# A decoder layer on eight cores: DMAs and side work placed by modelled PE time instead of where they are issued

## Chip, cores, metric

One Trainium2 chip, two dies of four cores; all eight cores run the same program on different data (two cores share a sequence of 4096 tokens, each produces 2048 output tokens). The metric is the device time of the slowest core, in microseconds (us). Some executions fall in a slower state, in which the cores of one die or of both show a lower granted clock.

PE is TensorE, DVE VectorE, ACT ScalarE, POOL GpSimd, SP the SyncE queue that issues plain DMAs. `ws` is the scratch copy of the weights in bf16, `wst` the fp32 original, one *unit* 128 x 2048 elements.

## The reference, cut to what matters

```python
h = rmsnorm(x, norm_mix_pre)
q, k, v, u, g_attn, g_pool = split(h @ w_in)
y_attn = stick_breaking_attention(q, k, v) @ w_attn_branch      # strictly causal, 8 heads of 128
y_pool = (pool_group(multiscale_causal_pool(u)) * pool_scale) @ w_pool_branch
x = x + rmsnorm((sigmoid(g_attn) * y_attn + sigmoid(g_pool) * y_pool) @ w_out, norm_mix_post)
h = rmsnorm(x, norm_ffn_pre)
gate, val = split(causal_depthwise_conv(h @ w_up))              # width 3: needs two earlier tokens
x = x + rmsnorm((gelu(gate) * val) @ w_down, norm_ffn_post)
x = x + rmsnorm(sigmoid(x @ w_ple_gate) * (p @ w_ple), norm_ple_post)
```

## The kernel before

A core works through four stages, which I call A to D. **A**: eight chunks of 512 tokens are normed, transposed and projected to K and V (chunks 4 to 7, its own, to Q too); with chunks 5 to 7 the attention of its first tile is interleaved, which begins with a *halo*, the attention of just two earlier tokens, needed by the convolution. **B**: four mixers (gates, branches, pooling, output projection), interleaved with the attention of the next tile. **C**: FFN up and down, twice. **D**: the per-layer embedding (PLE).

A small tracker in Python records which instruction last wrote or read each region and emits semaphore waits. In the traces an instruction that waits holds all that its engine has queued behind it: in the prediction's lines a norm's small step on POOL stands behind weight conversions, and PE waits 298 us for it. Small chains (norm, transpose, residual) lie in a list `side` and are popped after so much modelled PE time.

The parts that matter, with cuts:

```python
# weights: fp32 -> bf16, DRAM to DRAM, all 88 early units at the start, four to a DMA; POOL issues them
conv_units(list(range(U_V, U_U)), 4)
conv_units(list(range(U_U, U_UP)), 4)          # s_cv is a ring of 8 semaphores: the 9th waits for the 1st
def rstd(c_in, c_out):                         # part of every norm, on POOL too
    P.op("pool", ... tensor_scalar ...); P.op("pool", ... pow ...)

# end of the V projection of a chunk: V shifted by one row, minus V
P.dma("sp", s_v[0], [(Vs[0:127], Vv[1:128]), ...])
for hh in range(2):
    P.op("dve", ... Vsh - Vb ...)              # DVE's queue waits here for the copy

# halo: the load is issued at its use
for h in range(NH):
    kb_ = ldk(cc, h)
    P.op("pe", lambda e: e.matmul(bank(b), qh..., kb_.v(), ...), reads=[kb_.r(), qh.r()], ...)

# output projection, last block of a column group
for q_, ns in enumerate(mmq(pieces, [s[1].r() for s in sl] + [mxT.r()], [bkr(b)])):
    if lastb:
        W.done(sl[q_][0])                      # frees slot q_ and at once issues the next load into it
    yield ns                                   # ... but the next quarter declares all four slots as read
```

## Time and profile before

| | before |
|---|---|
| median of 16 runs | 6075.4 us |
| fast runs, all rounds | 6025 to 6112 us |
| cores of the profiled run | 6029.0 to 6081.7 us, clock 0.866 to 0.873 |
| PE busy | 4509.1 us, 74% of the span |
| stage A (to the last matmul before the first mixer) | 1736 us |
| stage B (to the first FFN matmul) | 1916 us |
| stage C (to the last FFN matmul) | 2037 us |
| stage D (rest) | 393 us |

How to read it: PE's work fills 74%, so a quarter of the time is waits, and the question is what each is for. The stage bounds are the first or last instructions of the source lines that belong to the stage. The lines are in the prediction.

### The profile page before, as it was taken

Reading aid. Unit: us, or ns where it says so; the run is one execution under the profiler, and the core shown is the slowest. Engines: PE = TensorE matmul, PEld = TensorE weight load, DVE = VectorE, ACT = ScalarE, POOL = GpSimd, SP = SyncE. Lnnn points to the kernel's source line nnn. Section 1 sums busy time; section 2 is a strip of 40 time slices with the busy share of each in tenths; the row PEclk is TensorE's granted clock in tenths of the full one; section 3 lists DMA queues with packets and bytes.
Section 4 is the critical chain, followed back from the end, with each engine's and each line's share of the span. In section 5 each row is a group of like instructions: output and inputs, shape, how many; then the busy total and the mean of one; then the engine's idle time right before and its main releaser. Section 6 shows DMA issues by size and latency. Waiting matters only on the chain.

```text
span 6081.7 us, 73291 instructions; the slowest of 8 cores (6029.0 to 6081.7 us)
## 1 busy us (share of the span) xinstructions
PE 4509.1 (74%) x25250; PEld 2351.5 (39%) x25664; DVE 2279.7 (37%) x2149; ACT 1855.4 (31%) x3066; POOL 220.4 (4%) x494
## 2 busy tenths in 40 slices
PE   1012645455779968967986867999988899998588
PEld 0001322223437624534543324666443344443233
DVE  0000211114747628847872214444221444411133
ACT  1000111103646526635762103333111333311122
POOL 1000000000000000000000000000000011100000
PEclk7566877778989979989997988999999999999697
DMA  9994223433357747746665833222454222247554
GB/s 165 109 110 85 67 65 112 142 112 123 113 148 187 176 123 195 188 129 187 179 170 147 199 114 117 74 77 77 139 191 159 91 77 77 77 144 211 145 152 132
DMA packets 328143, 803.31 MB, mean 132 GB/s; under 512 B 94826, under 2 KB 207914, under 8 KB 306090
## 3 DMA queue, kind: packets, MB, share of 16 engines
q1 hardware_dynamic: 317140, 663.02, 34.6%
q0 software_dynamic: 10640, 135.57, 15.7%
q8 instruction: 213, 3.49, 0.2%
q14 instruction: 150, 1.23, 0.1%
HBM read 823.40 MB, written 217.58 MB: 171 GB/s over the span
## 4 chain that ended last, share of the span: by engine, by line
PE 62%; DMA 18%; another core or an unknown queue 7%; SPq 5%; DVE 4%; issue 3%; ACT 2%; POOL 0%; DVEq 0%; ACTq 0%; POOLq 0%
PE PS L420 25%; PE PS L1239 20%; PE PS L1289 8%; SPq L202 4%; DMA SB<-ws 4%; DMA SB<-SB 3%; DMA SB<-xr 3%; PE PS L801 2%; PE PS L763 2%; PE PS L834 2%; DMA SB<-X 2%; DMA SB<-DVS 2%; DMA X<-SB 1%; DVE SB L519 1%
## 5 line engine op out<-in xcount | busy, mean ns | idle before, releaser
L420 PE MATMUL PS<-SB 128*128 128x512 bf16 (+3 forms) x9427 | 2131.4, 373 | 344.5 <-DMA SB<-ws 176.7
L420 PEld LDWEIGHTS PS<-SB 128*128 128x128 bf16 x9656 | 915.7, 101 | 1223.3 <-issue 596.3
L1239 PE MATMUL PS<-SB 128*128 128x342 bf16 (+1 forms) x6982 | 1227.6, 337 | 33.1 <-DVE SB L1034 29.9
L691 DVE TENSOR_TENSOR_SCAN SB<-SB 128x512 bf16<-128x512 f32 (+1 forms) x836 | 972.2, 1200 | 183.2 <-ACT SB L774 137.5
L439 ACT ACTIVATE SB<-PS 128x512 bf16<-128x512 bf16 (+5 forms) x1017 | 610.5, 605 | 1397.5 <-PE PS L534 430.0
L1239 PEld LDWEIGHTS PS<-SB 128*128 128x128 bf16 x7040 | 684.1, 97 | 574.6 <-issue 33.5
L534 PE MATMUL PS<-SB 128*128 128x128 bf16 x1024 | 94.0, 264 | 874.8 <-DVE SB L519 749.3
L1289 PE MATMUL PS<-SB 128*128 128x512 bf16 x2757 | 627.8, 388 | 26.8 <-DMA SB<-ws 12.6
L513 ACT ACTIVATE SB<-SB 128x512 bf16<-128x512 f32 (+3 forms) x245 | 216.9, 885 | 1386.6 <-DVE SB L443 815.0
L443 DVE COPY SB<-PS 128x512 f32<-128x512 f32 (+3 forms) x197 | 135.0, 687 | 1105.9 <-PE PS L1289 493.7
L774 ACT ACTIVATE SB<-PS 128x512 f32<-128x512 f32 (+1 forms) x832 | 475.4, 573 | 127.9 <-PE PS L763 64.0
L1263 DVE SCALAR_TENSOR_TENSOR SB<-SB 128x1024 f32<-128x1024 f32 x176 | 226.2, 1285 | 640.2 <-ACT SB L1256 640.2
L519 DVE SCALAR_TENSOR_TENSOR SB<-SB 128x2048 f32<-128x2048 f32 (+2 forms) x98 | 229.9, 2346 | 622.7 <-POOL SB L508 619.3
L534 PEld LDWEIGHTS PS<-SB 128*128 128x128 bf16 x1024 | 83.5, 121 | 895.0 <-issue 888.3
L1289 PEld LDWEIGHTS PS<-SB 128*128 128x128 bf16 x2816 | 280.5, 100 | 370.7 <-issue 76.6
L1253 ACT ACTIVATE SB<-PS 128x1026 f32<-128x1026 f32 (+1 forms) x176 | 180.5, 1025 | 744.0 <-PE PS L1239 737.9
L763 PE MATMUL PS<-SB 128*128 128x512 bf16 (+3 forms) x809 | 302.7, 376 | 124.7 <-ACT SB L774 66.2
L801 PE MATMUL PS<-SB 128*128 128x128 bf16 x3136 | 317.1, 222 | 3.7 <-DVE SB L691 1.4
L834 PE MATMUL PS<-SB 128*128 128x512 bf16 (+3 forms) x916 | 300.1, 351 | 24.6 <-DMA SB<-DVS 21.7
L801 PEld LDWEIGHTS PS<-SB 128*128 128x128 bf16 x3136 | 246.6, 99 | 180.8 <-issue 18.6
L1266 DVE SCALAR_TENSOR_TENSOR SB<-SB 128x1024 f32<-128x1024 f32 x176 | 226.1, 1285 | 19.1 <-DVE SB L1263 0.9
L443 DVE CAST SB<-PS 128x512 bf16<-128x512 f32 (+2 forms) x151 | 97.7, 649 | 340.0 <-PE PS L420 241.1
(53 smaller groups left out, 1393.8 us busy)
## 6 DMA issues: line engine op xcount, KB each, us to landing
SB<-ws SPq DMA_DIRECT2D x696, 512.0 KB, 3.7
ws<-wst POOLq DMA_DIRECT2D x66, 1024.0 KB, 10.3
SB<-xr SPq DMA_DIRECT2D x48, 1024.0 KB, 5.8
ws<-wst POOLq DMA_DIRECT2D x22, 2048.0 KB, 154.8
X<-SB SPq DMA_DIRECT2D x32, 1024.0 KB, 4.8
SB<-X SPq DMA_DIRECT2D x32, 1024.0 KB, 7.9
SB<-KS SPq DMA_DIRECT2D x240, 128.0 KB, 3.8
SB<-DVS SPq DMA_DIRECT2D x240, 128.0 KB, 3.8
```

What stands on the lines that cost most here:

```text
L202: e.dma_start(out=o, in_=i).then_inc(h, 16)
L420: ins = e.matmul(o, l, r, start=(start and a + i == 0), stop=(a + i == n - 1), skip_group_check=True)
L439: P.op("act", lambda e: e.activation(out=dst, in_=src, func=AF.Copy), reads=reads, writes=writes)
L443: P.op("dve", lambda e: e.tensor_copy(dst, src), reads=reads, writes=writes)
L519: P.op("dve", lambda e: e.scalar_tensor_tensor(out=dst, in0=xv, scalar=cv, in1=gv, op0=ALU.mult, op1=ALU.mult), reads=[xr_, small.r(col, c ...
L691: P.op("dve", lambda e: e.tensor_tensor_scan(out=pb.v(lo, NT), data0=gb.v(lo, NT), data1=mask, initial=init, op0=ALU.mult, op1=ALU.max), r ...
L763: P.op("pe", lambda e: e.matmul(bank(bk, NT - lo, lo), q_.v(b_ * 128, (b_ + 1) * 128), kb_.v(lo, NT), start=True, stop=True), reads=[kb_.r ...
L774: P.op("act", lambda e: e.activation(out=gb.v(lo, NT), in_=bank(bk, NT - lo, lo), func=AF.Sigmoid, scale=-QSCALE), reads=[bkr(bk)], writes ...
L801: ins = e.transpose(at[:, q_ * 128:(q_ + 1) * 128], src[q_].v(kb * 128, (kb + 1) * 128), ident)
L834: ins = e.matmul(o_, l, r, start=(first and i == 0), stop=False, skip_group_check=True)
L1239: ins = e.matmul(bank(bs[bi], c1 - c0), w3[:, k, :], hT2v[:, k, c0:c1], start=(k == 0), stop=(k == 15), skip_group_check=True)
L1289: ins = e.matmul(bank(b), actb[kk].v(q_ * 512 + blk * 128, q_ * 512 + (blk + 1) * 128), w3[:, k, :], start=(kk == 0), stop=(kk == NF - 1), ...
```

## The change

Its intent is to let PE run without holes, by giving each DMA and each side instruction a place in modelled time. The arithmetic is the same. The core of the diff (cuts are marked; memory layout and renaming are left out):

```diff
+        def after(ns, f, reads=(), writes=()):        # f is emitted ns of modelled PE time later; until
+            h = Hold(...)                             # then a conflicting access makes it fire first
+            timers.append((now[0] + ns, ...))
+        def dma_after(ns, q, sem, pairs, reads, writes):
+            after(ns, lambda: P.dma(q, sem, pairs, reads=reads, writes=writes), reads, writes)
...
-        conv_units(list(range(U_V, U_U)), 4)
-        conv_units(list(range(U_U, U_UP)), 4)
+        conv.extend(range(U_V, U_UP, 2))
+        def conv_every(ns, due=None):                 # two units, gated on PE's present count
+            if conv:
+                convert(conv[0], conv[0] + 2, ("pe", P.esem["pe"], P.cnt["pe"]))
+                conv.popleft()
+                after(due + ns - now[0], lambda: conv_every(ns, due + ns))
+        conv_every(11500)                             # 25000 in the mixers, 20000 from FFN up on
...
-            P.dma("sp", s_v[0], [(Vs[0:127], Vv[1:128]), ...
+            P.dma("sp", s_v[0], [(Vs[0:112], Vv[1:113]), (Vs[112:127], Vv[113:128]), ...
+            after(2000, t1, ...); after(11000, t2, ...); after(16500, t3, ...)   # copy, subtract, store
...
-                    for q_, ns in enumerate(mmq(pieces, [s[1].r() for s in sl] + [mxT.r()], [bkr(b)])):
+                    for q_, ns in enumerate(mmq(pieces, lambda a, sl=sl: [sl[a // 4][1].r(), mxT.r()], [bkr(b)])):
...
+        load_h2(0)                                    # FFN's input is loaded before the last mixer,
+        stats.append(run(mixer(3)))                   # and FFN up follows it without a drain
...
-                    P.dma("sp", s_st[4], [(H3[tb], st.v())], ...)    # FFN no longer transposes for PLE;
+            after(12000, lambda: tr3(n, xb), writes=[h3seq[n].r()])  # PLE does, one block ahead
-            P.dma("pool", s_wg[cg], [..., wsrc[cg])], ...)           # gate weights cast at their load
+            P.dma("sp", s_wg[cg], [..., ws[U_PG + cg * 4:...])], ...) # converted earlier
```

Besides, x loads run two blocks ahead, K, Q and residual stores are issued by `dma_after`, and `att_total` gets the true length of the attention, so that it ends with its mixer.

## The prediction

> **What bounds the kernel now.** I read the cores first: 6029.0 to 6081.7 us on all eight, clock 0.866 to 0.873, both dies alike, so this is the fast state. Then the page's head and slices.
>
> ```profile
> span 6081.7 us, 73291 instructions; the slowest of 8 cores (6029.0 to 6081.7 us)
> PE 4509.1 (74%) x25250; PEld 2351.5 (39%) x25664; DVE 2279.7 (37%) x2149; ACT 1855.4 (31%) x3066; POOL 220.4 (4%) x494
> ...
> PE   1012645455779968967986867999988899998588
> PEclk7566877778989979989997988999999999999697
> DMA  9994223433357747746665833222454222247554
> ```
>
> PE is the busiest engine, but only 74%, and each slice (152 us) in which it is low also has a low clock. The first eleven slices are poor, the middle is mixed, the end is good but for two dents. So this is no kernel with one bound; I asked for stretches instead.
>
> ```profile
> 50.00:660.00 610.00, 134.03 (x662) 64.27 (x675) 36.94 (x34) 33.24 (x41) 12.95 (x30) 0.61 0.81 104
> 660.00:1090.00 430.00, 222.38 (x1223) 107.71 (x1243) 63.32 (x67) 56.35 (x71) 9.64 (x26) 0.76 0.30 97
> 1090.00:1736.00 646.00, 395.55 (x2296) 194.90 (x2343) 238.50 (x229) 203.96 (x384) 5.19 (x14) 0.80 0.35 114
> ...
> 3750.00:4355.00 605.00, 592.23 (x4029) 389.95 (x4029) 264.80 (x208) 224.87 (x208) 15.45 (x83) 0.99 0.27 85
> ```
>
> (Columns: stretch, length, busy PE, weight loads, DVE, ACT, POOL, clock, DMA share, GB/s.) The projection phase up to 660 us has DMA at 0.81 and PE at a fifth; from there to 1736 us neither is full, so something serialises them; FFN up is PE-bound at full clock. The timeline of POOL, then of PE, names the first hole:
>
> ```profile
> 43.83 4.06 POOL L202 DMA_DIRECT2D ws<-wst  x8
> 109.50 0.51 POOL L202 DMA_DIRECT2D ws<-wst  x1 [61.62 <-DMA ws<-wst]
> 128.47 0.50 POOL L202 DMA_DIRECT2D ws<-wst  x1 [18.46 <-DMA ws<-wst]
> ...
> 360.70 0.50 POOL L202 DMA_DIRECT2D ws<-wst  x1 [18.73 <-DMA ws<-wst]
> 361.27 0.19 POOL L506 TENSOR_SCALAR SB<-SB 128x1 f32<-128x1 f32 x1
> ```
>
> ```profile
> 364.95 1.86 PE L534 MATMUL PS<-SB 128*128 128x128 bf16 x16 [298.20 <-DVE SB L519]
> 525.33 1.87 PE L534 MATMUL PS<-SB 128*128 128x128 bf16 x16 [130.12 <-DVE SB L519]
> ```
>
> 22 weight conversions (fp32 to bf16, DRAM to DRAM, 2 MB written each) share eight semaphores, so POOL stands at the ninth until the first has landed. The tiny rstd of chunk 1's norm (L506) is behind them in POOL's queue; norm, transpose and PE wait 298 us. The second hole, 130 us, is an x load of 102.9 us behind the last eight conversions. The list of waits has the rest:
>
> ```profile
> DVE SB L645 <- DMA SB<-SB: 350.7, 8, 47.6
> ...
> PE PS L420 <- DMA SB<-ws: 176.7, 48, 7.7
> ```
>
> The first is the copy that shifts V by one row, 8 times 44 us: DVE's queue stands at it, the next chunk's norm behind it, and PE has holes of 47, 47, 49, 69 us and so on. The second is 48 = 4 mixers x 4 column groups x 3: the code frees a weight slot after each quarter of the last block and refills it at once, but the next quarter still declares all four slots as read, so PE waits 3 to 8 us for a load that it doesn't need.
>
> **What the Trainium skill says.** "DMA: Bandwidth & Descriptors", section "Why a DMA increments its semaphore by 16 and not by 1": a DMA is spread over the largest k up to 16 that divides the slowest dimension; 127 partitions go to one engine. The trace agrees: the 127-row shift takes 44 us where the 128-row store of as many bytes (DVS) lands in 6.3 us. The same page, "Queues, rings and completion order": each engine alternates between queues packet by packet. The trace shows what that gives here: conversion packets average 12.7 KB (135.57 MB in 10640), the others 2.1 KB, and a 1 MB x load took 103 us instead of 5.8. "TensorE: Matmul & The Clock Gate", Part 1, says that an idle array falls to half clock (agrees: mean 0.61 in the holes) and that a peak-current limiter holds 13/16 once three cores of a die run dense matmuls. The trace disagrees: from 3800 to 4300 us all eight cores were PE-busy 500.00 of 500.00 us at clock 1.00.
>
> **The change, part by part.** The arithmetic stays. What is new: every store, load and conversion is put at a point of modelled PE time instead of where its producer was issued; conversions are two units each, one per 11.5 us of PE time (25 in the mixers, 20 in FFN up), gated on PE's count; x loads are prefetched two blocks ahead; the shift is 112+15 rows; slots are waited for and freed singly; the attention share of the merge is recomputed; H3 goes (PLE reads X2 and transposes itself); FFN's layout lets FFN up start while the last mixer's tail runs; the PLE gate is converted beforehand.
>
> Unit costs from the trace: a 512-column matmul in a dense run 10.74/49 = 0.219 us; a 342-column one 580.77/3992 = 0.1455; a transposed block 1.05; an attention unit 0.65 (2400 to 2580 us: 180 us less 512 dense matmuls, over about 104 units). A conversion of 2 MB takes 19 us, so 110 GB/s at share 1.00, and one of two units 9.5. Plain DMA: 70 GB/s at share 0.22, about 320 at full share (estimate).
>
> *A, to 1736 us.* PE: 2560 matmuls x 0.219 = 561, 32 blocks 34, attention 148 units 96, halo about 20, start 50: 760. DMA: 190 MB moved (the rates above by their lengths), of which 44 x 1.05 + 8.4 = 54.5 MB cast: 54.5/0.110 + 135/0.320 = 495 + 422 = 917 us; the shares give 898, which agrees. So the POOL, x and shift holes (298, 130 and some 350 us) go, but not all becomes gain: DMA becomes the bound. While conversions last, 12.6 us of PE (11.5 plus transposes) meet 9.5 us of conversion and about 7 of other traffic. 917 plus a tenth for moments when prefetch buffers are full and no conversion is in flight: 1000. Gain 736.
>
> *B, mixers, 1736 to 3652.* Four times (1152 x 0.219 + pool, group and transposes 14) = 267, mixer 0's halo 27, attention 1 to 3: 636 units x 0.65 + 6 = 420; sum 1515. These ran at 98 to 99% PE with one conversion per 24 us or so already, so DMA is no bound. Add 60: four boundaries, mixer 0's first loads (14 us now), attention's ends. 1575; gain 341, 177 of it from the false slot waits, the rest from attention ending with its mixer, and cold clock.
>
> *C, FFN, 3652 to 5689.* 4224 x 0.1455 = 615; 5632 x 0.219 = 1235; 1850 in all, plus 22 for starts and four blocks. 1872; gain 165: first the 30 us hole at 3622 and transposes between 3652 and 3741, which stall PE because H2 and norm chains are in line with FFN up, then the same pattern at 4681 to 4741 and in the down stages, where a transposed block waits for its add and cast.
>
> *D, PLE, 5689 to 6082.* 1152 x 0.219 = 253, 12 blocks 13, 14 of tail as now, 5 for the first gate weights: 285; gain 108, which is the 27.6 us wait for H3, three 7 to 17 us transposes and two-thirds clock.
>
> Sum: 1000 + 1575 + 1872 + 285 = 4732; I say 4730.
>
> **Rivals.** 1. *Conversions starve the SP queue still.* Every one gates HW traffic for 9.5 us, and POOL, which carries rstd, now also waits for PE counts: a late conversion delays a norm, which delays PE, which delays the next conversion. For it: the 103 us x load. Against: there eight were in flight, here about one, and 40 mixer conversions didn't hurt. If true, A is 1150 to 1250 and the time 4900 to 5000. 2. *DMA overlaps fully* (A at 850, for PE time plus starting loads): 4580. For it: backlog of eight conversions may trail the PE. Against: 917 us of packet time in the same bytes. 3. *The limiter*: if PE at 90% and more for 4 ms brings the clock to 0.81, dense parts stretch by 1.23 and the time is about 5400; the 500 us windows at 1.00 on all cores speak against it. 4. *New in-order waits*: a timer placed by modelled time fires too early, and SP's single queue stands at a store whose producer is late, with weight loads behind it. Worth some 100 us, most likely in A, where real time runs behind the model.
>
> **Range and chances.** A carries the doubt (850 to 1200), B some 50, C and D 30 together. Small waits that I can't see add rather than subtract, but the sum of PE work alone is 4410, so there is no room far below. Range 4540 to 4970. Even rival 3 gives over 10%: faster 0.98, same 0.01, slower 0.01.
>
> **What would show it.** A right: no PE hole over 20 us after 120 us, DMA share 0.85 or more until the conversions end, the mixer starting near 1000 us; the shift landing in under 8 us. B right: the L420 wait for ws (48 times) nearly gone and PE over 95% to the end of mixer 3. C right: FFN up directly behind the mixer, no hole over 10 us, clock 1.00. D right: under 300 us. Wrong if PE has holes of tens of us behind POOL or an x load in A (rival 1), if A's DMA share is under 0.75 with A long (rival 4), or if the clock is under 0.95 in FFN (rival 3).

## The result, and the profile after

The changed kernel took 4986.84 us (median of 11 runs; fast runs 4974 to 4993), before 6075.4. The ratio of the fast runs is 0.8217, interval 0.8198 to 0.8237. Ratios here are the mean time of one kernel's fast runs over that of the other's in the same rounds, so they are not quite the ratio of the medians quoted. The gain is large, but the time is 17 us above the top of my range and 257 above the value.

The head and slices of the page of the changed kernel:

```profile
span 4991.0 us, 73809 instructions; the slowest of 8 cores (4945.6 to 4991.0 us)
PE 4417.4 (89%) x25664; PEld 2316.1 (46%) x25664; DVE 2278.4 (46%) x2149; ACT 1845.7 (37%) x3066; POOL 244.8 (5%) x520
...
PE   5886545797999899899979899999999999999988
PEclk9998768899999999999989999999999999999999
DMA  9799655756776766777464655546464222247642
```

PE is at 8 or 9 tenths nearly everywhere. What is left is one dent, slices 4 to 7, that is 370 to 870 us. In the busy stretches by stage it looks like this (columns as in the prediction):

```profile
50.00:530.00 480.00, 357.88 (x1936) 172.17 (x1936) 104.55 (x103) 92.26 (x115) 30.36 (x70) 0.87 0.90 181
530.00:900.00 370.00, 204.10 (x934) 84.03 (x934) 44.17 (x43) 34.57 (x47) 12.71 (x25) 0.76 0.59 148
900.00:1150.00 250.00, 208.70 (x1396) 112.18 (x1394) 194.83 (x185) 165.92 (x334) 2.95 (x6) 0.94 0.65 161
...
2815.00:3440.00 625.00, 608.35 (x4160) 404.93 (x4159) 295.63 (x231) 239.05 (x222) 35.23 (x126) 0.98 0.52 133
```

Until 530 us the DMA engines are 0.90 busy and PE 0.75 (before, in its first stretch to 660 us: 0.81 and 0.22). From 530 to 900 us neither is full: 0.59 and 0.55. FFN up was PE-bound before and is now.

The POOL queue, where the 298 us hole was born:

```profile
116.66 0.50 POOL L202 DMA_DIRECT2D ws<-wst  x1 [15.19 <-PE PS L468]
127.93 0.49 POOL L202 DMA_DIRECT2D ws<-wst  x1 [10.77 <-PE PS L468]
140.04 0.49 POOL L202 DMA_DIRECT2D ws<-wst  x1 [11.62 <-PE PS L468]
```

A conversion every 11 to 12 us, each released by PE (L468 is the matmul helper) and not by the conversion eight before. From the list of waits (who waited for whom, total us, times, longest):

```profile
DVE SB L719 <- DMA SB<-SB: 91.7, 4, 41.9
...
PE PS L782 <- DMA SB<-KS: 80.3, 16, 13.0
...
PE PS L822 <- DMA SB<-DVS: 48.3, 13, 12.4
...
PE PS L468 <- DMA SB<-HC: 22.7, 1, 22.7
PE PS L822 <- DMA SB<-VS: 19.1, 3, 12.6
...
PE PS L468 <- DMA SB<-ws: 2.1, 2, 1.1
```

The shift's 350.7 us became 91.7, the false slot wait's 176.7 became 2.1. The shift is not cured while conversions run, though: of its four remaining waits the longest is 41.9 us, and it makes the largest hole of PE in A. SP, DVE and PE there:

```profile
355.34 40.79 SPq L202 DMA_DIRECT2D SB<-SB  x4
404.01 2.55 DVE L719 TENSOR_TENSOR SB<-SB 128x2048 bf16<-128x2048 bf16 x2 [41.90 <-DMA SB<-SB]
410.50 1.86 PE L588 MATMUL PS<-SB 128*128 128x128 bf16 x16 [32.74 <-DVE SB L573]
```

SP needs 40.8 us to issue the four pieces (DMA share 0.94 in these 41 us), the subtraction on DVE stands for the copy, the next norm (L573) behind it, and PE behind that.

The L782 and L822 lines are the halo: 147.7 us in which PE stands at loads of K, DV and V. L782 in the timeline of PE:

```profile
632.98 0.58 PE L782 MATMUL PS<-SB 128*128 128x512 bf16 x1 [8.38 <-DMA SB<-KS]
639.67 0.59 PE L782 MATMUL PS<-SB 128*128 128x512 bf16 x1 [4.41 <-DMA SB<-KS]
650.06 0.58 PE L782 MATMUL PS<-SB 128*128 128x512 bf16 x1 [6.39 <-DMA SB<-KS]
```

One matmul of 0.58 us, preceded by 4 to 8 us of idle PE, again and again: each load is issued when its matmul is, and PE waits for it to land (median of all K loads, 4.7 us from issue to landing).

By stages, with the same bounds as before:

| stage | before | predicted | measured | off by |
|---|---|---|---|---|
| A | 1736 | 1000 | 1135 | +135 |
| B | 1916 | 1575 | 1652 | +77 |
| C | 2037 | 1872 | 1908 | +36 |
| D | 393 | 285 | 296 | +11 |
| sum | 6082 | 4732 | 4991 | +259 |

### The profile page after: what moved, and what is told of

Same layout as the page of the kernel before. It is cut to its first block, busy times and chain, and to the rows that moved or that the text cites. A ratio compares the mean times of both kernels' runs of the same rounds, so it can differ in the third digit from the quotient of the medians.

```text
span 4991.0 us, 73809 instructions; the slowest of 8 cores (4945.6 to 4991.0 us)
## 1 busy us (share of the span) xinstructions
PE 4417.4 (89%) x25664; PEld 2316.1 (46%) x25664; DVE 2278.4 (46%) x2149; ACT 1845.7 (37%) x3066; POOL 244.8 (5%) x520
## 4 chain that ended last, share of the span: by engine, by line
PE 76%; DMA 12%; SPq 4%; DVE 3%; issue 2%; ACT 2%; POOL 0%; DVEq 0%; ACTq 0%; POOLq 0%
PE PS L468 31%; PE PS L1303 23%; PE PS L1354 11%; SPq L202 4%; DMA SB<-DVS 4%; PE PS L913 3%; PE PS L842 3%; PE PS L880 3%; DMA SB<-KS 2%; DVE SB L573 1%; PE PS L588 1%; DMA KS<-SB 1%; DMA SB<-X 1%; DMA SB<-ws 1%; DMA X<-SB 1%
## 5 line engine op out<-in xcount | busy, mean ns | idle before, releaser
L468 PE MATMUL PS<-SB 128*128 128x512 bf16 (+2 forms) x9656 | 2077.8, 363 | 121.0 <-DVE SB L491 36.7
L468 PEld LDWEIGHTS PS<-SB 128*128 128x128 bf16 x9656 | 899.6, 99 | 939.5 <-issue 217.3
L487 ACT ACTIVATE SB<-PS 128x512 bf16<-128x512 bf16 (+4 forms) x1017 | 609.3, 604 | 1174.5 <-PE PS L468 411.9
L1303 PEld LDWEIGHTS PS<-SB 128*128 128x128 bf16 x7040 | 684.1, 97 | 555.6 <-issue 13.9
L1354 PE MATMUL PS<-SB 128*128 128x512 bf16 x2816 | 612.7, 380 | 11.9 <-DMA SB<-ws 11.8
L1354 PEld LDWEIGHTS PS<-SB 128*128 128x128 bf16 x2816 | 275.6, 98 | 346.8 <-issue 19.0
L913 PE MATMUL PS<-SB 128*128 128x512 bf16 (+1 forms) x960 | 313.8, 350 | 44.0 <-DMA SB<-DVS 36.0
L842 PE MATMUL PS<-SB 128*128 128x512 bf16 (+1 forms) x832 | 308.8, 373 | 30.3 <-DMA SB<-KS 16.9
L880 PEld LDWEIGHTS PS<-SB 128*128 128x128 bf16 x3136 | 243.2, 98 | 176.8 <-issue 11.9
L880 PE MATMUL PS<-SB 128*128 128x128 bf16 x3136 | 313.4, 220 | 3.7 <-ACT SB L487 2.6
L573 DVE SCALAR_TENSOR_TENSOR SB<-SB 128x2048 f32<-128x2048 f32 (+2 forms) x98 | 229.8, 2345 | 116.4 <-POOL SB L562 92.2
L588 PE MATMUL PS<-SB 128*128 128x128 bf16 x1024 | 82.5, 244 | 191.3 <-DVE SB L573 171.9
L1320 ACT ACTIVATE SB<-PS,SB 128x1026 f32<-128x1026 f32 (+1 forms) x176 | 212.1, 1205 | 37.4 <-DMA X<-SB 20.8
```

The costliest lines, as they stand in the source:

```text
L468: ins = e.matmul(o, l, r, start=(start and a + i == 0), stop=(a + i == n - 1), skip_group_check=True)
L487: P.op("act", lambda e: e.activation(out=dst, in_=src, func=AF.Copy), reads=reads, writes=writes)
L573: P.op("dve", lambda e: e.scalar_tensor_tensor(out=dst, in0=xv, scalar=cv, in1=gv, op0=ALU.mult, op1=ALU.mult), reads=[xr_, small.r(col, c ...
L842: P.op("pe", lambda e: e.matmul(bank(bk, NT - lo, lo), q_.v(b_ * 128, (b_ + 1) * 128), kb_.v(lo, NT), start=True, stop=True), reads=[kb_.r ...
L880: ins = e.transpose(at[:, q_ * 128:(q_ + 1) * 128], src[q_].v(kb * 128, (kb + 1) * 128), ident)
L913: ins = e.matmul(o_, l, r, start=(first and i == 0), stop=False, skip_group_check=True)
```

## The experiments

Theory 1: A is late because the halo's loads are issued at their use. Theory 2: A is late because the sum of DMA work bounds it. (Rival 1 of the prediction, that conversions in flight hold up SP's queue, would look much like theory 2, and no run below was built to tell the two apart.) To see where a variant moves, I use two milestones of its profiled core: a copy that each mixer makes once, in mixer 0 some 60 us after its first matmul ("mixer"), and the first FFN matmul ("FFN"). One core is good to some 20 us: in the changed kernel the eight cores have the mixer at 1187 to 1214 us, and FFN minus mixer at 1554 to 1576. Where a difference is that small, the mean of the eight cores is given. Rounds differ too: the median fast run of the kernel before was 6038 to 6051 us in the four rounds of experiments.

| kernel | ratio to before, fast runs | mixer at | FFN at | FFN minus mixer |
|---|---|---|---|---|
| before | 1 | 1812.6 | 3652.7 | 1840 |
| changed | 0.8217 | 1213.7 | 2786.9 | 1573 |
| changed, halo loads ahead (core of the fast die) | 0.8101 | 1127.4 | 2684.6 | 1557 |
| changed, early conversions per 17 us | 0.8506 | 1194.5 | 2943.8 | 1749 |
| changed, shift of 127 rows | 0.8680 | 1478.1 | 3052.7 | 1575 |
| changed, four slots waited for | 0.8598 | 1216.0 | 2984.5 | 1769 |
| changed, one chain of conversions per 18.5 us | 0.8164 | 1146.4 | 2736.9 | 1591 |
| changed, all halo loads and mixer 0's ahead | 0.8041 | 1100.6 | 2661.6 | 1561 |
| the last two together | 0.7960 | 1024.1 | 2610.6 | 1587 |
| before, shift split alone | 0.9552 | 1543.4 | 3385.5 | 1842 |
| before, conversions paced alone | 0.9667 | 1590.2 | 3433.4 | 1843 |
| before, these two and single slots (core of the fast die) | 0.8836 | 1284.3 | 2918.2 | 1634 |

### 1. The halo's loads ahead of their use

```diff
-                        kb_ = ldk(cc, h)
+                        kb_ = kbs[n_ % 9]              # 3 K buffers + 6 idle ones; loads run 8 ahead
...
-                        dv = lddv(cc, h)
+                        dv = dbs[n_ % 7]               # 4 + 3 buffers; loads run up to 7 ahead
```

> The changed kernel, but the 32 K, 32 DV loads of the two-row halo attention are issued up to 8 and 7 steps ahead (spare buffers) instead of at use. Theory 1 (stage A is late because PE stands 4 to 13 us at each halo load issued at its use, 166 us of idle PE between 530 and 900 us): those waits vanish, the mixer starts 90 to 140 us earlier, 4850 to 4900 us. Theory 2 (A is late because the 16 DMA engines are full, as the prediction had it): the same bytes at the same time, 4960 to 5000 us.

Fast runs 4895 to 4909 us, ratio 0.8101: some 76 us faster than the changed kernel's median fast run, and the mixer comes 86 us earlier. Theory 1 stands, but for less than I expected. The stretches of a core of the undisturbed die (the profiled run fell in the slow state on the other one):

```profile
530.00:900.00 370.00, 233.79 (x1294) 111.09 (x1295) 97.70 (x95) 79.56 (x138) 14.67 (x29) 0.81 0.85 193
900.00:1060.00 160.00, 147.00 (x1036) 80.76 (x1034) 139.97 (x135) 121.13 (x244) 0.98 (x2) 0.98 0.53 155
```

The time is at the slow edge of theory 1's 4850 to 4900. The DMA share from 530 to 900 us rose from 0.59 to 0.85. With the loads ahead, the engines are nearly as full there as in the stretch before, so the halo's waits had kept DMA idle too, and DMA is the next limit to look at.

### 2. Fewer conversions in A

```diff
-        conv_every(11500)
+        conv_every(17000)
```

> The changed kernel with the early conversions one per 17 us of modelled PE time instead of 11.5 (same 44 conversions, all still before the mixer). Theory 1 (halo loads issued at use, conversions only lengthen some): chunks 1 to 4 get faster by some 40 us, the halo gets no better since more conversions now fall in it; 4940 to 4990 us. Theory 2 (A bound by the sum of DMA work): the sum is unchanged, so within 15 us of 4987. A third (conversions collide with x loads and stores, so bunching them costs): 4880 to 4930 us, the holes of 14, 33, 23 and 15 us before 535 us gone.

5146 to 5151 us, slower by 166: a miss for all three theories, and the fault of my edit. In A it did gain: the mixer came 19 us earlier. But 44 conversions at 17 us don't end within A's modelled time, and the chain, which lives as long as the list isn't empty, ran on beside the mixers' own chain of 25 us. POOL in mixer 0 of this run:

```profile
1218.41 0.49 POOL L202 DMA_DIRECT2D ws<-wst  x1 [23.95 <-PE PS L468]
1234.64 0.49 POOL L202 DMA_DIRECT2D ws<-wst  x1 [15.74 <-PE PS L468]
1236.61 0.49 POOL L202 DMA_DIRECT2D ws<-wst  x1 [1.48 <-PE PS L468]
```

and its waits:

```profile
PE PS L913 <- DMA SB<-DVS: 201.7, 35, 15.8
```

L913 is the attention's second matmul; in the changed kernel it waits 36.0 us for DVS in all, here 201.7. So a conversion per 10 us or so (two chains of 17 and 25) is too much for the mixers, at 25 us it isn't. The right test is one chain:

```diff
-        conv.extend(range(U_V, U_UP, 2))
-        conv_every(11500)
+        conv.extend(range(U_V, U_D, 2))
+        conv_every(18500)                             # and no second chain in the mixers
```

> The changed kernel with one chain of all 88 conversions, one per 18.5 us of modelled PE time through stage A and the three mixers (11.5 in A and 25 in the mixers before; the 17 us run was spoiled because its chain ran on beside the 25 us chain). About ten conversions, 95 us of full DMA, move from A to the mixers. Theory 2 (A is bound by the sum of DMA work): A shorter by 60 to 95 us, mixers unchanged or 20 us longer, 4900 to 4940 us. Theory 1 (only the halo's loads issued at use count): 4950 to 4985 us.

4939 to 4943 us, ratio 0.8164: 42 us faster than the changed kernel. (The ratio's interval, 0.8097 to 0.8231, includes the changed kernel's 0.8217, since one fast run of before in this round took 6112 us; the gain is read from the times and the milestones.) The mixer comes 67 us earlier, and the mixer stage takes 17 us longer (64 and 14 in the means of the eight cores). So 35 conversions in A instead of 44, some 86 us of DMA at full share, free A of about 65: that is what theory 2 says. But it is also what rival 1 says. The five holes of PE of over 9 us before 540 us, three behind a shift and two behind K or Q stores, 96 us together, became four with 54, and SP issued the shift that had taken it 40.8 us in 17.2. The run doesn't tell whether fewer bytes or a freer queue made the gain.

### 3. Both, and the mixer's first loads

The first try combined the halo prefetch and the loads of mixer 0 (its h and context, issued one chunk earlier) with the faulty 17 us pace:

> The changed kernel with halo prefetch, conversions one per 17 us, and the mixer's first h and context loads issued one chunk earlier (a 22.7 us hole at 1135 us). Theory 1: 4810 to 4870 us. Theory 2: the DMA work of stage A is unchanged, 4930 to 4980 us (only the 22.7 us hole goes).

5022 and 5036 us in the fast runs, ratio 0.8312: the doubled chain of conversions again, so it says nothing of the theories. With the pace of the change, V loads ahead too, and DV loads running across the chunk boundary:

> The changed kernel with halo K, DV and now also V loads issued ahead (DV across the chunk boundary too), and the mixer's first loads one chunk earlier; conversions as in the change. Theory 1: 85 us as measured for the first prefetch, 22 for the mixer's first loads, 20 to 40 for V and DV: 4830 to 4870 us. Theory 2 (DMA share in the halo was 0.85 already in the first prefetch run): only the mixer's loads count, 4865 to 4885 us.

4865 to 4870 us, ratio 0.8041: 116 us faster than the changed kernel. That lies in both ranges, at the slow end of theory 1's and the fast end of theory 2's, so the time doesn't choose. The mixer comes 113 us earlier: 86 as in the first prefetch, and the rest is about the HC hole of 22.7 us at mixer 0's start, which is gone from the trace; V loads, and DV loads across the boundary, brought little. And with the single chain of conversions:

> The previous kernel with the one chain of conversions at 18.5 us. If A is then bound by DMA, moving conversions out pays more here than without prefetch: 4740 to 4800 us. If the moved conversions slow the mixers as much as they free A: 4830 to 4870 us.

4815 to 4823 us, ratio 0.7960. The mixer comes at 1024.1, 190 us before the changed kernel's, so A ends near 965 us (the copy comes some 60 us after the mixer's start). Neither expectation was met exactly: A gained 77 more, and the mixers gave 25 of it back.

### 4. Single parts undone and done

The shift as 127 rows again in the changed kernel:

```diff
-[(Vs[0:112], Vv[1:113]), (Vs[112:127], Vv[113:128]), ...
+[(Vs[0:127], Vv[1:128]), ...
```

> The changed kernel with the V shift as one copy of 127 rows again. If the split is what removed the 44 us DVE stalls: 8 stalls of 25 to 40 us come back (the copy has 9 us of modelled lead), most of it on PE's path: 5130 to 5250 us. Rival (deferring the subtract by a timer was enough, or DMA is the bound anyway): below 5040 us.

5231 to 5291 us, at the slow end of what I expected and above it, ratio 0.8680; the mixer 264 us later, all else as it was. Its wait of DVE for the copy is 267.5 us in five:

```profile
DVE SB L719 <- DMA SB<-SB: 267.5, 5, 74.9
```

A timer of 9 us does not help against a copy of 44. That the copy runs on one DMA engine can be seen in the kernel before. In 21 us in which it is the only transfer, the DMA share is 0.06, one sixteenth, at 27 GB/s:

```profile
673.00:694.00 21.00, 0.00 (x0) 0.00 (x0) 0.00 (x0) 0.00 (x0) 0.00 (x0) 0.50 0.06 27
```

The reverse, the split in the kernel before:

> The kernel before with the V shift as 112 + 15 rows only. Theory (127 rows run on one DMA engine; DVE's queue stands behind): each of six stalls of 46 us after 560 us shrinks to about 8, chunk time 108 to 70 us; 5780 to 5860 us. Rival (the time is SP's issue or another wait that takes its place): above 5950 us.

5778 and 5782 us, ratio 0.9552; the mixer 269 us earlier, and DVE's eight waits for the copy fell from 350.7 to 73.1 us. Undoing and doing agree.

The four slots declared as read again in the changed kernel:

```diff
-lambda a, sl=sl: [sl[a // 4][1].r(), mxT.r()]
+[s[1].r() for s in sl] + [mxT.r()]
```

> The changed kernel, but the last block of the output projection again declares all four weight slots as read while it frees them one by one. If this false wait was worth its 176.7 us before: 48 waits of about 3.7 us return, 5130 to 5180 us. Rival (attention now runs to the end of each mixer and its matmuls lie between, so the refill lands in their shadow): for three of four mixers half of it is hidden, 5040 to 5100 us.

5182 to 5238 us, above both ranges, ratio 0.8598; A unchanged, the mixer stage 195 us longer (200 in the mean of the eight cores).

```profile
PE PS L468 <- DMA SB<-ws: 162.6, 48, 7.9
```

The wait is back with its 48 times, and it costs some 30 us more than its own length. The attention's matmuls that lie between hid nothing of it, so the rival failed. The reverse:

> The kernel before with this one part of the change: the output projection waits for one weight slot at a time. Theory (48 false waits, 176.7 us, all PE idle): 5890 to 5930 us (before: 6075). Rival (the mixers' weights come no faster, so PE waits for the next real load instead): above 6000 us.

No run of it was fast. In one the second die was hardly disturbed (clock 0.885 to 0.887), and its cores took 5819 to 5852 us, against 6024 to 6042 for the same die in a fast run of before: 201 us less, more than I expected. The 48 waits are gone:

```profile
PE PS L420 <- DMA SB<-ws: 3.0, 1, 3.0
```

The conversions paced alone in the kernel before (two units per 11.5 us of modelled PE time, the rest flushed at the end of chunk 6):

> The kernel before with the early conversions paced only: two units per 11.5 us of modelled PE time, gated on PE's count, instead of 22 of four units at the start. Theory (the 298 and 130 us holes are POOL's queue behind its ninth conversion, then an x load behind eight of them): both holes go, chunks 1 and on cost 20 to 40 us more each while conversions run beside them; 5700 to 5850 us. Rival (conversions are DMA work that has to be paid anyway in this stage): above 5950 us.

5826 to 5861 us, ratio 0.9667; the mixer 222 us earlier. It would be more without a hole of 88 us at 1195 us, in which PE waits for DVS, as I read it behind the conversions that my edit flushes at once.

All three in the kernel before:

> The kernel before with three parts together: single slot waits (about 205 us alone, from the undisturbed die), split shift (270 alone), paced conversions (210 alone). Additive: 5350 to 5400 us, so that these three are two thirds of the whole gain. If the shift's stalls were partly hidden behind the conversion holes, the three together give more than their sum: 5200 to 5300 us. If DMA becomes the bound in stage A: 5450 to 5550 us.

Fast runs 5326 to 5402 us, ratio 0.8836, between "more than their sum" and "additive"; on the better die, 5293 to 5329 us. The mixer comes 528 us earlier (269 + 222 = 491 alone), although PE has a hole of 84 us for DVS here too. The core shown is the earliest; in the mean of the better die the mixer comes 516 us earlier, and the mixer stage is 208 us shorter. In means over cores, the change won 610 us up to the mixer milestone and 277 from there to FFN. So these parts give 516 of 610 and 208 of 277, and the rest of the change, with the whole machinery of timers, buys some 95 and 70 there, and what C and D gained.

### 5. A wait that the change brought in

B was 77 us over. The trace of the changed kernel shows at the last mixer's start, on DVE:

```profile
2491.42 0.69 DVE L491 CAST SB<-PS 128x512 bf16<-128x512 f32 x1 [2.61 <-PE PS L913]
2519.86 0.18 DVE L1282 COPY SB<-SB 128x32 bf16<-128x32 bf16 x1 [27.75 <-DMA SB<-H]
```

FFN's input is now loaded there, and a copy of two columns into it makes DVE's queue stand 27.75 us; PE has a hole of 23.0 us at 2507.7. The copy 30 us of modelled time later:

```diff
-                P.op("dve", lambda e: e.tensor_copy(hT2v[:, :, 1024:1026], ...), ...)
+                after(30000, lambda: P.op("dve", ...), [h2h.r()], [hT2.r()])
```

> The changed kernel, but the small DVE copy of two halo columns into FFN's input is issued 30 us of modelled time later. If DVE's queue standing 27.8 us at this copy (behind the load of FFN's input) makes the 23 us PE hole at the start of the last mixer: 4955 to 4970 us and the hole gone. Rival (the hole belongs to the third mixer's norm tail, which ends then anyway): 4978 to 4990 us.

One fast run of six, 4967.25 us, so there is no interval; that is 15 below the changed kernel's median fast run (4982), but the round was a little faster for the kernel before too. The milestones decide: from the mixer to FFN it took 1546 us instead of 1564 in the mean of the eight cores, 18 us less. The PE hole shrank from 23.0 to 15.4 us. In the fastest version:

> The fastest version so far (4816 us) with the same late copy: 4790 to 4803 us if the hole is the copy's; 4812 to 4820 us if it is the norm tail's.

One fast run of six, 4801.12 us, against 4815 to 4823; from the mixer to FFN 1564 us instead of 1579, by the same means. Both times lie in the range for "the hole is the copy's", with some 15 us of it, though the hole didn't go as expected. In B of the changed kernel PE was busy 1522 us, near the 1515 of the prediction's sum, and waited 130 instead of the 60 allowed: 23.0 for this copy, 22.7 for the HC load, which belongs to B by my bounds, and the rest in many waits under 10 us that no experiment took apart.

## Why the prediction was right or wrong

It was wrong in its size: 4986.84 against a top of 4970. By its steps:

- **The holes named in A** were right. The 298 and 130 us holes are gone with paced conversions, and most of the shift's stalls with the split (264 and 269 us by undoing and doing). The x load no longer starves for 100 us.
- **The step that failed is A's overlap, "917 plus a tenth".** The prediction let DMA be the bound through the whole of A, with 83 us for moments without it. The two sums of work were near: PE was busy 778 us of A (760 predicted), and DMA had about 850 (share 0.75 of 1135 us, against 917). (The prediction's plain rate, 70 GB/s at share 0.22, reads 76 at 0.23 in FFN up of before; its 917 would then be 904.) But 284 us, not 83, came on top of DMA's work. The largest piece is the halo, from 530 to 900 us, where neither engine was full (PE 0.55, DMA 0.59): its loads are issued at their use, and PE stood 147.7 us at them. The sum has only work for it, "halo about 20". Loads ahead of use gave back 86 us of A's 135. The profile of before showed the wait, in the halo's first and second matmul:

```profile
PE PS L703 <- DMA SB<-KS: 91.2, 13, 53.2
...
PE PS L743 <- DMA SB<-DVS: 27.3, 8, 4.9
```

Of the 91.2 us, 53.2 are one wait. The prediction put the halo down as work and didn't carry the waits into the sum.
- **"DMA becomes the bound"** was half right. Until 530 us the share is 0.90, as predicted (0.85 or more), but the conversions went on to about 980 us, and from 530 to 900 it was 0.59. Moving nine conversions out freed about 65 us. A's 1000 was reached only by a version that removes the halo's waits as well and defers conversions, near 965; with the halo's waits gone alone, A ended near 1040.
- **Rival 1** came in part. POOL's small steps did not stand behind conversions. But its first half did come, conversions that hold up SP's queue: the sign "the shift landing in under 8 us" failed with waits of 16.3, 23.5 and 41.9 us, and "no PE hole over 20 us" with 32.7 and 23.0. The time fell into the band that the prediction gave to this rival, 4900 to 5000; since the rival says nothing of the halo, that agreement is luck.
- **Rival 3, the limiter,** did not come: FFN up is at 0.98 to 1.00. **Rival 4** came in small: the subtraction and the copy at 2519.86, both placed by modelled time or program order before their data had landed, the copy for some 15 us. Its sign, A's share under 0.75, was just missed at 0.75.
- **B** was right in its largest part, the false wait: 195 and 201 us by undoing and doing, against 177 in my sum. But the allowance of 60 was too small: besides the HC load and the copy, PE has many short waits; 1652 against 1575, with PE busy 92% and not over 95%.
- **C and D** came within 2 and 4% in time, and PE has no hole of 10 us in C; their parts were not tested one by one.
- **The range** was too narrow: its top, 4970, cut through the band of its own rival 1. Stage sums built from PE rates with small allowances all erred to the same side: +135, +77, +36, +11.

## What to carry to other kernels

When work moves to a new bound, add up the waits that the old profile already shows in that stage, not only the work; loads issued at their use held PE for 147.7 us here, in a stretch where neither PE nor DMA looked busy. Before building a scheduler, look for waits that a single line causes: three such lines (a row count that doesn't divide, a dependency that is too wide, a burst in a queue that also carries small work) made most of this gain. When pacing a stream, check that the old pacer has stopped.

## What the Trainium skill lacked or had wrong

- "TensorE: Matmul & The Clock Gate", "Seeing it yourself", states a limiter at 13/16 of the clock as soon as three cores of a die run dense matmuls. In the fast run profiled before the change all eight cores were PE-busy for 500 us at clock 1.00, with this case's data. In slow runs a whole die is low, as the page has it for the limiter, yet only in some executions of the same kernel: mean clock 0.771 to 0.774 on one die and 0.889 to 0.893 on the other in one run of the split shift alone.
- "DMA: Bandwidth & Descriptors", "Why a DMA increments its semaphore by 16 and not by 1", agrees with the runs on how many engines a DMA gets: 127 rows took 44 us, at a DMA share of 0.06 where nothing else moved, and the split into 112 and 15 rows took 269 us off the kernel before. What I didn't find there is how long the issuing queue stands. SP spent 19 to 23 us in issuing the three pieces of the 127-row shift in the kernel before, 3 to 4 us on the four pieces of the split there, and 41 us on such four pieces when the engines were 0.94 busy.
- The same page, "Queues, rings and completion order", says that engines alternate by packets. I found no page with the consequence for a casting copy: conversions from DRAM to DRAM ran at 110 GB/s with the engines at share 1.00 (plain DMA about 330 GB/s, an estimate from 76 GB/s at share 0.23 in FFN up), and beside eight of them a 1 MB load took 103 us.
